# A router chain in program order, its second parts on VectorE, and one modulation sixth moved into it

## The chip, the cores and the metric

One core of a Trainium2 chip runs the whole program. The metric is the device time of one execution in microseconds; the median of three runs before the change is 961.68 us (961.64, 961.68 and 965.34). All arithmetic is float32; "fp32r" in a row marks a float32 operand that TensorE takes in its reduced form, so a value is split into a high part and a remainder and multiplied twice.

## The reference, cut to what matters

Two layers act on 256 latent tokens of width 1024. Layer 0 mixes with attention and a recurrent unit, layer 1 with a Hyena operator (filters applied by Fourier transforms). In each layer the vector `c` gives six modulation vectors, each one sixth of `silu(c) @ ada_w + ada_b`: shift, scale and gate of the mixer (0, 1, 2) and of the expert stage (3, 4, 5). After each mixer comes a mixture of 16 experts:

```
h = rms_norm(x, g) * (1 + sc2) + sh2
s = sigmoid(h @ router_w)            # 16 scores for each token
sel = s + router_b                   # best group of 4, then the best 2 in it
y = sum_e gates[e] * (silu(h @ w1[e]) * (h @ w3[e])) @ w2[e]
x = x + g2 * y
```

## The kernel before, in words

**Stages.** The mixer of layer 0 ends with `project_out` (L501), whose four last steps each finish a quarter of `x`. Between these steps the class `router` (L540) squares, transposes and multiplies the finished quarters. Then comes `moe(0)` (L1171), the Hyena mixer of layer 1 (L1558 on), the second router and `moe(1)`.

**The chain of the router.** `enter` takes the sum of squares and the transposed quarter, `weights` multiplies it with the router's weights, `norm` makes the reciprocal root (a chain of small VectorE instructions, `rstd_of`), `logits` finishes the scores. `split` (L634) writes the normed tokens as a high part `yh` and a remainder `yl`: ScalarE makes `yh` and a full copy, GpSimd subtracts the two. `choose` (L656) finds the two experts of each token by comparisons on VectorE, `count` (L675) numbers the tokens of each expert with small matmuls, `place` (L1197) makes the matrix `P` that picks tokens, and `gather` (L1207) multiplies `yh` and `yl` with `P`. Only then can `up` (L1241) start with the first experts.

**Expert weights.** One expert has six tiles of 1 MB, 96 tiles a layer. They are loaded from SyncE's queue (SP), which issues in order: each load waits until its buffer is free. The buffers are a ring of nine (`w`), which the mixers' and the modulation's weights use as well, the tiles `sp` that the mixers leave free, and an extra pool `x`. The order of loading is the list that `plan` fills (L206 to L308); `emit` issues from it ahead of use.

**The modulation sixths.** `ada_step` (L408) does one of eight steps of a sixth. By PLAN a half goes to VectorE ("V", eight instructions at L440 and L442) or to TensorE ("P", L433, sixteen instructions of the trace a half, and one copy at L437). Its four weight tiles stay in the ring until the last step that reads them. `ada_columns` (L367, for shifts and scales) or `ada_row` (L381, for gates) then finish it on TensorE. `bg(n)` takes n steps beside other work; sixth (1, 4) runs in the mixer of layer 0, (1, 2) and (1, 5) in the Hyena mixer.

**Order.** A planner that simulates the program puts each engine's instructions in order, except inside `in_order("...")`, where the engines named keep the order of the program. Before, that holds for ScalarE and VectorE during `choose` and the second `split` (L623 to L626, CH is 2).

Of the kernel before, what the change touches and what calls it, by code (L numbers as in the profile page):

```python
# [17 lines left out]
D = 1024  # L18
KD = 8
# [41 lines left out]
FILLS = 40  # L61
PLAN = {(0, 3): "VV", (1, 2): "VV", (1, 5): "VV"}
TIN = 0
ADAP = (1, 2, 3, 5)
BGP = (0, 0, 1, 1, 1, 1)

# [100 lines left out]
def build(tc, A, dbg=None, stop=None):  # L167
# [130 lines left out]
    for n in range(6):  # L298
        if n in EARLY:
            plan_moe(1, EARLY[n])  # L300
        for kk in range(2):
            plan(("odin", n, kk), mat(A["od_w_in"][0], kk * 512, 4, n * 512, 512), (128, 4, 512))
        for i in range(4):
            if ADAP[i] == n:
                plan_ada(1, 2 if i < 2 else 5, (i % 2,))
# [96 lines left out]

    todo, ripe, current, ada_alloc, part = [], [], [], [None], [None]

# [3 lines left out]
    def ada_step():  # L408
        for r in ripe:
            r[0] += 1  # L410
        if ripe and ripe[0][0] > LAG:
            l, s, use, e = ripe.pop(0)[1]
            for hf in range(2):
                if use == "row":
                    ada_row(l, s, hf, e[:, hf, :])
                else:
                    ada_columns(l, s, hf, use, e[:, hf, :], ones, 1)
        if not current:
            if not todo:
                return bool(ripe)  # L420
            current.extend([todo.pop(0), 0, ada_alloc[0]("e", 2, 512)])
        (l, s, use), k, e = current
# [3 lines left out]
        for hf in range(2):  # L426
            eh = e[:, hf, :]
            if on[hf] == "P":
                if k == 3:
                    part[0] = ps()  # L430
                if k % 4 == 3:
                    for q in range(4):
                        T.matmul(part[0][32 * q:32 * q + 32, :], cs[:, k - 3 + q, :],  # L433
                                 get(("ada", l, s, hf, k // 4))[:, q, :], start=(k == 3), stop=(k == 7),
                                 tile_position=(0, 32 * q))
                if k == 7:
                    S.activation(eh, part[0], AF.Copy)  # L437
# [12 lines left out]
        if current[1] == KD:  # L450
            if use == "row":
                for hf in range(2):
                    r = l * 12 + s * 2 + hf
                    V.scalar_tensor_tensor(e[0:24, hf, :], adab, ident[0:24, r:r + 1], e[0:24, hf, :], op0=OP.mult,
                                           op1=OP.add)
            ripe.append([0, (l, s, use, e)])
            current.clear()
# [82 lines left out]
    class router:  # L540
# [34 lines left out]
        def weights(self, i):  # L575

            t, n = divmod(i, 2)
            if n == 0:
                self.p[t] = ps()
            for k in range(4):  # L580
# [12 lines left out]
        def run(self, out):  # L593

            self.weigh()
            next(out)
            for i in range(4):
                if i == 2:
                    self.norm(0)
# [5 lines left out]
                if i == 2:  # L605
                    self.logits(0)
            self.norm(1)
            self.weights(3)
            self.logits(1)
            self.y = [eight(n, 2, D, dt=F32R) for n in ("yh", "yl")]  # L610
            if CH == 0:
                self.choose()
                self.split(0)
                self.split(1)
            elif CH == 1:
                self.split(0)
                in_order("A")
                self.choose()
                self.split(1)
                in_order()  # L620
            elif CH == 2:
                self.split(0)
                in_order("AD")  # L623
                self.choose()
                self.split(1)
                in_order()  # L626
            elif CH == 3:
                in_order("A")
                self.choose()
                self.split(0)  # L630
                self.split(1)
                in_order()

        def split(self, t):  # L634

            yh, yl = self.y
            for n in range(2):
                c = slice(n * 512, n * 512 + 512)
                S.activation(yh[:, t, c], x[:, t, c], AF.Copy, scale=self.r[t])
                v = self.alloc()  # L640
                S.activation(v, x[:, t, c], AF.Copy, scale=self.r[t])
                G.tensor_tensor(yl[:, t, c], v, yh[:, t, c].bitcast(F32), op=OP.subtract)

# [12 lines left out]
        def choose(self):  # L656
# [75 lines left out]
        def gates(self):  # L732

            s, msk, gate, sm = self.s, self.msk, self.gate, self.sm
            V.tensor_tensor(gate, s, msk, op=OP.mult)
            V.tensor_reduce(sm[:, 2, 0:2], gate, axis=mybir.AxisListType.X, op=OP.add)
# [38 lines left out]
    with ExitStack() as pa:  # L775
# [38 lines left out]
        later(1, 3, "sh")  # L814
        later(1, 4, "sc")

# [334 lines left out]
        bg_all()  # L1151
        dump("x1", x)

# [17 lines left out]
    def moe(l, route, ws, filler=None, fills=((0, 0, 0),) * 8, budget=0, late=None, prepare=None, finish=None):  # L1171
# [4 lines left out]

        in_order(ORDER[1 + 2 * l])
        steps = filler(wk, f2) if filler else iter(())
        next(steps, None)
        sc, sh, gate, (yh, yl) = route.sc, route.sh, route.gate, route.y  # L1180
# [25 lines left out]

        def gather(d, plan):  # L1207

            P = place_[d]
            e = xe[d] = wk.tile([128, KD, 256], F32, tag="xe", name=nm("xe"))  # L1210
            w = 128 * len(plan[2 * d:2 * d + 2])
            for k2 in range(4):
                p = ps()
                for kk in range(2):
                    k = 2 * k2 + kk
                    for i in range(4):
                        t = i // 2
                        T.matmul(p[:, kk * w:kk * w + w], (yl if i % 2 else yh)[:, t, k * 128:k * 128 + 128],  # L1218
                                 P[:, t, :w], start=(i == 0), stop=(i == 3))
                k = 2 * k2  # L1220
# [102 lines left out]
        place(0, route.pos, firsts)  # L1323
        route.gates()
        gather(0, firsts)
        route.sort(w2("srt"))
# [231 lines left out]
    later(1, 2, "row")  # L1558
    later(1, 5, "row")
    with ExitStack() as ph:  # L1560
# [209 lines left out]
```

## Time and profile before

| | |
|---|---|
| median of three runs | 961.68 us |
| the profiled execution | 964.56 us, span 962.8 us |
| TensorE (PE) busy | 868.0 us, 90% |
| VectorE (DVE) busy | 477.8 us, 50% |
| ScalarE (ACT) busy | 231.9 us, 24% |
| GpSimd (POOL) busy | 25.9 us, 3% |
| moved by DMA | 289.33 MB, mean 301 GB/s |
| mean granted TensorE clock | 0.961 |

All durations in the rows come from this one execution. Times are from the span's start. The mixer of layer 0 ends near 258 us, its experts near 540, the Hyena mixer near 704, the experts of layer 1 at the end. A DMA share of 1.0 means that the core's 16 DMA engines were busy all the time. A clock of 1.0 is 2.4 GHz, 0.5 is 1.2 GHz.

### The profile page before, as it was taken

To read this page: it belongs to the slowest core of one execution; us is meant where nothing else is said; L and a number is where in the kernel's file an instruction comes from. 1 tells how busy PE (TensorE), PEld (TensorE's weight loads), DVE (VectorE), ACT (ScalarE), POOL (GpSimd) and SP (SyncE) were. 2 spreads that over 40 slices of the span, in tenths; PEclk is the share of its full clock that TensorE was granted. 3 is DMA by queue.
4 is the path that set the end of the run, shared out by engine and by line. 5 is a ranking of instruction groups with operands and counts; after the bars stand their busy time and mean duration, and the time that the engine had idled before them with its cause. 6 is when DMAs were issued, how large, how long until landed. Compare 5 with 4: busy or idle time off the path is not lost. (4 is left out here: it accounts for less than half of the span.)

```text
span 962.8 us, 10887 instructions
## 1 busy us (share of the span) xinstructions
PE 868.0 (90%) x3992; PEld 458.1 (48%) x3992; DVE 477.8 (50%) x1119; ACT 231.9 (24%) x451; POOL 25.9 (3%) x29
## 2 busy tenths in 40 slices
PE   3898999999969999889999599999959999988984
PEld 1445755575543543433343288677545352422431
DVE  5349775763364445345622469976163241322123
ACT  3266414430231222122211312211031020100112
POOL 0000000000010000001100000000020000000000
PEclk9899999998969999999999799999978999999997
DMA  9946679469479889999999866842285999999994
GB/s 353 336 183 240 224 263 354 166 223 367 170 271 324 333 324 386 383 400 396 391 362 347 308 228 253 314 167 88 87 298 189 391 396 386 401 392 396 396 386 148
DMA packets 130568, 289.33 MB, mean 301 GB/s; under 512 B 6828, under 2 KB 8876, under 8 KB 130500
## 3 DMA queue, kind: packets, MB, share of 16 engines
q1 hardware_dynamic: 129428, 286.39, 81.5%
q10 hardware_dynamic: 1072, 2.10, 0.7%
q8 instruction: 35, 0.57, 0.2%
q14 instruction: 33, 0.27, 0.1%
HBM read 287.42 MB, written 1.05 MB: 300 GB/s over the span
## 5 line engine op out<-in xcount | busy, mean ns | idle before, releaser
L1247 PE MATMUL ps<-w,xe 128*64 128x512 f32 (+1 forms) x696 | 174.3, 597 | 2.8 <-DMA w<-in_moe_w 2.8
L1247 PEld LDWEIGHTS ps<-w,xe 128*64 128x64 f32 (+1 forms) x696 | 50.0, 129 | 88.0 <-issue 79.2
L1275 PE MATMUL ps<-w,at 128*64 128x512 f32 (+1 forms) x344 | 87.1, 597 | 4.5 <-DMA w<-in_moe_w 2.7
L1591 PE MATMUL ps<-xt,w 128*128 128x256 f32 x384 | 88.2, 388 | 1.8 <-ACT xt L1554 1.8
L1591 PEld LDWEIGHTS ps<-xt,w 128*128 128x128 f32 x384 | 74.2, 195 | 14.4 <-ACT xt L1554 2.1
L1294 DVE TENSOR_TENSOR x<-x,ps 128x512 f32<-128x512 f32 x56 | 37.0, 684 | 68.1 <-PE ps L1292 68.1
L442 DVE SCALAR_TENSOR_TENSOR e<-w,sg,e 128x512 f32<-128x512 f32 x91 | 67.0, 746 | 5.2 <-DMA w<-in_ada_w 4.1
L1281 DVE SCALAR_TENSOR_TENSOR ye<-ps,gs,grow 128x512 f32<-128x512 f32 x28 | 21.0, 748 | 83.9 <-PE ps L1275 83.9
L1247 PE MATMUL ps<-sp,xe 128*64 128x512 f32 (+1 forms) x216 | 55.5, 600 | 1.5 <-DMA sp<-in_moe_w 1.5
L1275 PEld LDWEIGHTS ps<-w,at 128*64 128x64 f32 (+1 forms) x344 | 26.9, 130 | 50.8 <-issue 40.3
L1283 ACT ACTIVATE yeh<-ye 128x512 fp32r<-128x512 f32 x28 | 17.6, 630 | 118.2 <-DVE ye L1281 118.2
L1257 DVE TENSOR_TENSOR th<-th,ps 128x512 f32<-128x512 f32 x14 | 9.6, 688 | 60.5 <-PE ps L1247 60.5
L1247 PE MATMUL ps<-x,xe 128*64 128x512 f32 (+1 forms) x112 | 37.5, 596 | 1.6 <-DMA x<-in_moe_w 1.6
L1218 PE MATMUL ps<-P,yh 128*128 128x256 f32 (+1 forms) x128 | 35.9, 313 | 2.8 <-DVE P L1203 2.8
L1218 PE MATMUL ps<-P,yl 128*128 128x256 f32 (+1 forms) x128 | 35.0, 307 | 0.0
L1223 ACT ACTIVATE xe<-ps,modc 128x256 f32<-128x256 f32 (+1 forms) x32 | 16.5, 540 | 70.0 <-DVE xe L1221 69.9
L1218 PEld LDWEIGHTS ps<-P,yh 128*128 128x128 f32 x128 | 27.9, 218 | 9.6 <-issue 7.1
L844 PE MATMUL ps<-hT,w 128*128 128x512 f32 x64 | 31.0, 643 | 1.2 <-DMA w<-in_ev_w_in 1.2
L1247 PEld LDWEIGHTS ps<-sp,xe 128*64 128x64 f32 (+1 forms) x216 | 16.0, 132 | 28.1 <-issue 24.4
L510 PE MATMUL ps<-w,x 128*128 128x512 f32 x64 | 28.4, 595 | 0.7 <-ACT x L1605 0.7
L510 PE MATMUL ps<-w,mix 128*128 128x512 f32 x64 | 28.8, 598 | 0.0
L1218 PEld LDWEIGHTS ps<-P,yl 128*128 128x128 f32 x128 | 27.8, 217 | 1.7 <-issue 1.7
(350 smaller groups left out, 1313.9 us busy)
## 6 DMA issues: line engine op xcount, KB each, us to landing
w<-in_moe_w SPq DMA_DIRECT2D x126, 1024.0 KB, 13.8
w<-in_ada_w SPq DMA_DIRECT2D x48, 1024.0 KB, 7.1
sp<-in_moe_w SPq DMA_DIRECT2D x41, 1024.0 KB, 14.2
x<-in_moe_w SPq DMA_DIRECT2D x21, 1024.0 KB, 14.5
w<-in_od_w_in SPq DMA_DIRECT2D x12, 1024.0 KB, 7.1
w<-in_ev_w_in SPq DMA_DIRECT2D x4, 1024.0 KB, 11.0
w<-in_ev_w_out SPq DMA_DIRECT2D x4, 1024.0 KB, 6.8
w<-in_moe_w SPq DMA_DIRECT2D x8, 512.0 KB, 9.8
```

Source lines behind the costliest of these rows:

```text
L442: V.scalar_tensor_tensor(eh, w[hf], c, eh, op0=OP.mult, op1=OP.add)
L510: T.matmul(po[t][n], a[:, k, t * 128:t * 128 + 128], b[:, n * 512:n * 512 + 512], start=(k == korder[0] and i == 0), stop=(k == korder[-1] ...
L844: T.matmul(uxp[b], get(("wux", hf))[:, k % 4, b * 128:b * 128 + 128], hT[hf][:, k % 4, :], start=(k == 0), stop=(k == KD - 1))
L1218: T.matmul(p[:, kk * w:kk * w + w], (yl if i % 2 else yh)[:, t, k * 128:k * 128 + 128], P[:, t, :w], start=(i == 0), stop=(i == 3))
L1223: S.activation(e[:, k, :w], p[:, w:2 * w], AF.Identity, scale=sc[:, k:k + 1], bias=sh[:, k:k + 1])
L1247: T.matmul(p[room * i:room * i + room, :], xe[j // 2][:, k, o:o + room], weight(nme, e, k), start=(k == 0), stop=(k == KD - 1), tile_posit ...
L1257: V.tensor_tensor(act[j], act[j], hid[j, "w3"], op=OP.mult)
L1275: T.matmul(p[room * i:room * i + room, :], act[j][:, o:o + room], weight("w2", e, k, n), start=(k == 0), stop=(k == 3), tile_position=(0, ...
L1281: V.scalar_tensor_tensor(e, po[j, n], gs[j], grow[l, 5][:, n * 512:n * 512 + 512], op0=OP.mult, op1=OP.mult)
L1283: S.activation(h, e, AF.Copy)
L1294: V.tensor_tensor(xs, xs, p, op=OP.add)
L1591: T.matmul(pb, w[:, k % 4, b * 128:b * 128 + 128], hT[:, k, :], start=(k == 0 and b % 2 == 0), stop=(k == KD - 1 and b % 2 == 1))
```

## The change

The router's part from the second norm to the gather keeps program order on TensorE, ScalarE and VectorE (`in_order("PAD")`). GpSimd leaves it: `high` writes `yh` on ScalarE, and `low_` makes `yl` in one VectorE instruction for each quarter, the first token half while `count` runs on TensorE, the second behind `place`. `gather` takes all `yh` first and `yl` last, in four PSUM banks at once. The sigmoid's scaling is folded into the bias `rbh`. `gates` and the first step of `filters` move behind the gather. Sixth (1, 4) leaves the mixer of layer 0 and (1, 5) the Hyena mixer; each is now wholly on TensorE, inside the chain, in front of `count`, and finished behind the gather. Their weight tiles are loaded ahead of the experts' and keep four places of the ring until then.

```diff
-PLAN = {(0, 3): "VV", (1, 2): "VV", (1, 5): "VV"}
+PLAN = {(0, 3): "VV", (1, 2): "VV", (1, 4): "PP", (1, 5): "PP"}
-ADAP = (1, 2, 3, 5)
-BGP = (0, 0, 1, 1, 1, 1)
+ADAP = (1, 2)
+BGP = (0, 0, 1, 1, 0, 0)
...
     for k0 in range(0, 8, 2):
         plan(("odo", k0), mat(A["od_w_out"][0], k0 * 128, 2, 0, 1024), (128, 2, 1024))
+    plan_ada(1, 5)
     plan_moe(1)
...
+    rbh = kp.tile([128, 16], F32, name="rbh")
+    V.tensor_scalar(rbh, pc("rb", 0, 16), 0.5, None, op0=OP.add)
...
         def norm(self, t):
-            V.tensor_tensor(self.ss[:, 2 * t:2 * t + 1], self.ss[:, 2 * t:2 * t + 1], self.ss[:, 2 * t + 1:2 * t + 2],
-                            op=OP.add)
-            self.r[t] = rstd_of(self.ss[:, 2 * t:2 * t + 1], 1, D)
+            self.r[t] = rstd_of(self.ss[:, 2 * t + 1:2 * t + 2], 1, D, part=self.ss[:, 2 * t:2 * t + 1])
...
+            self.y = [eight(n, 2, D, dt=F32R) for n in ("yh", "yl")]
             self.norm(1)
+            self.high(0)
+            in_order("PAD")
             self.weights(3)
             self.logits(1)
...
+            S.activation(self.s, self.logit, AF.Tanh, scale=0.5)
+            self.high(1)
+            self.choose()
+
+        def high(self, t):
+            for n in range(2):
+                c = slice(n * 512, n * 512 + 512)
+                S.activation(self.y[0][:, t, c], x[:, t, c], AF.Copy, scale=self.r[t])
+
+        def low_(self, t):
+            for n in range(2):
+                c = slice(n * 512, n * 512 + 512)
+                V.scalar_tensor_tensor(self.y[1][:, t, c], x[:, t, c], self.r[t], self.y[0][:, t, c].bitcast(F32),
+                                       op0=OP.mult, op1=OP.subtract)
...
-            S.activation(s, self.logit, AF.Tanh, scale=0.5)
-            V.tensor_scalar(s, s, 0.5, 0.5, op0=OP.mult, op1=OP.add)
-            V.tensor_tensor(sel, s, pc("rb", 0, 16)[:, None, :].to_broadcast([128, 2, 16]), op=OP.add)
+            V.scalar_tensor_tensor(sel, s, 0.5, rbh[:, None, :].to_broadcast([128, 2, 16]), op0=OP.mult, op1=OP.add)
...
             p = ps()
+            self.low_(0)
             T.matmul(p[:, 0:16], tri, msk[:, 0, :], start=True, stop=True)
...
-        later(1, 4, "sc")
...
-    emit(5)
+    emit(9)
...
+            for i in range(4 if late_low else 0):
+                y_, t = (yh, yl)[i // 2], i % 2
+                for k in range(KD):
+                    T.matmul(pk2[k // 2][:, k % 2 * w:k % 2 * w + w], y_[:, t, k * 128:k * 128 + 128], P[:, t, :w],
+                             start=(i + k % 2 == 0), stop=(i == 3 and k % 2 == 1))
...
+        ada_alloc[0] = lambda n, *shape: [w2(n) for _ in range(2)]
+        later(*(1, 4, "sc") if l == 0 else (1, 5, "row"))
+        bg(KD)
         route.count()
         place(0, route.pos, firsts)
+        route.low_(1)
+        gather(0, firsts, True)
+        in_order(ORDER[1 + 2 * l])
+        next(steps, None)
+        bg_all()
         route.gates()
-        gather(0, firsts)
         route.sort(w2("srt"))
...
-    later(1, 5, "row")
...
-        emit(WHERE.index("x") - sum(EARLY.values()))
+        emit(4 + WHERE.index("x") - sum(EARLY.values()))
```

## Rows read from the trace of the kernel before

**Rows 1.** Busy time by stretch: length, engines with counts, clock, DMA share, GB/s

```profile
222.00:258.00 36.00, 36.00 (x141) 18.50 (x134) 9.13 (x18) 2.37 (x6) 0.00 (x0) 0.99 0.67 251
...
283.00:291.00 8.00, 8.00 (x41) 2.99 (x39) 0.31 (x2) 0.77 (x2) 0.00 (x0) 1.00 0.29 95
291.00:333.00 42.00, 41.82 (x216) 19.45 (x216) 19.48 (x51) 7.80 (x16) 1.71 (x2) 1.00 0.97 357
333.00:345.00 12.00, 12.00 (x59) 4.76 (x56) 3.63 (x9) 2.17 (x4) 0.00 (x0) 1.00 0.48 160
...
670.00:704.00 34.00, 34.00 (x120) 18.12 (x119) 8.72 (x16) 3.34 (x8) 0.00 (x0) 1.00 0.21 66
704.00:723.00 19.00, 8.66 (x62) 8.51 (x61) 14.82 (x68) 8.67 (x18) 5.10 (x4) 0.68 1.01 380
723.00:735.00 12.00, 12.00 (x61) 7.84 (x62) 4.88 (x19) 2.64 (x5) 0.00 (x0) 0.80 0.05 8
735.00:945.00 210.00, 193.30 (x942) 76.35 (x939) 54.43 (x106) 23.69 (x47) 0.00 (x0) 1.00 1.03 392
```

**Rows 2.** Waits, whole span: who waited for whom, us in total, times, longest

```profile
PE ps L679 <- DVE rg L673: 17.8, 2, 8.9
```

**Rows 3.** Timeline of the router chain of layer 1: start, length, engine, line, operation

```profile
709.48 0.23 DVE L590 SCALAR_TENSOR_TENSOR rg<-ps,rs,rwb 128x16 f32<-128x16 f32 x1
709.52 5.17 POOL L642 TENSOR_TENSOR yl<-xT,yh 128x512 fp32r<-128x512 f32 x4 [229.68 <-DMA w<-in_moe_w]
...
710.58 0.21 ACT L663 ACTIVATE rg<-rg 128x32 f32<-128x32 f32 x1
...
710.82 1.24 DVE L664 TENSOR_SCALAR rg<-rg 128x32 f32<-128x32 f32 x1 [1.10 <-ACT rg L663]
...
712.32 1.25 DVE L649 TENSOR_TENSOR cmp<-rg 128x128 f32<-128x128 f32 x1
...
714.76 0.28 DVE L652 TENSOR_TENSOR cmp<-cmp,kc 128x128 f32<-128x128 f32 x1
...
717.83 0.58 PE L679 MATMUL ps<-rg,kc 128*128 128x16 f32 x2 [8.92 <-DVE rg L673]
...
721.53 0.55 PE L1218 MATMUL ps<-P,yh 128*128 128x256 f32 x1 [1.42 <-DVE P L1203]
...
728.25 1.08 PE L1247 MATMUL ps<-sp,xe 128*64 128x512 f32 x4
```

**Rows 4.** Timeline of VectorE in the router chain of layer 0

```profile
267.01 0.29 DVE L649 TENSOR_TENSOR cmp<-rg 128x128 f32<-128x128 f32 x1
...
267.42 1.36 DVE L652 TENSOR_TENSOR cmp<-cmp,kc 128x128 f32<-128x128 f32 x1
```

**Rows 5.** Page, costliest groups: busy, mean ns, idle before

```profile
L442 DVE SCALAR_TENSOR_TENSOR e<-w,sg,e 128x512 f32<-128x512 f32 x91 | 67.0, 746 | 5.2 <-DMA w<-in_ada_w 4.1
```

**Rows 6.** Timeline of TensorE: first and next instruction of a later gather, layer 0

```profile
324.59 0.39 PE L1218 MATMUL ps<-P,yh 128*128 128x256 f32 x1
...
328.53 0.38 PE L1234 MATMUL ps<-kc,P 128*128 128x128 f32 x2
```

**Rows 7.** Timeline of TensorE at the end of the mixer of layer 0

```profile
230.33 1.92 PE L433 MATMUL ps<-w,cs 128*32 128x512 f32 x16
...
237.44 1.84 PE L370 MATMUL ps<-ones,e 128*128 128x1 f32 x16
```

**Rows 8.** Waits of TensorE, 300 to 545 us

```profile
PE ps L1247 <- DMA w<-in_moe_w: 1.9, 1, 1.9
PE ps L1275 <- DMA w<-in_moe_w: 1.3, 2, 0.7
```

**Rows 9.** Chain that ended last, 670 to 722 us: start, length, piece

```profile
676.03 1.72 PE ps L385 x4
```

**Rows 10.** Waits of TensorE, 545 to 705 us

```profile
PE ps L1495 <- DVE x L1665: 0.9, 1, 0.9
```

**Rows 11.** Timeline of SyncE's queue at the router of layer 0

```profile
259.28 8.20 SPq L219 DMA_DIRECT2D sp<-in_moe_w  x5
```

More of the change, by code (lines that the diff above doesn't have):

```diff
@@ L302, in build @@
             plan(("odin", n, kk), mat(A["od_w_in"][0], kk * 512, 4, n * 512, 512), (128, 4, 512))
-        for i in range(4):
+        for i in range(2):
             if ADAP[i] == n:
-                plan_ada(1, 2 if i < 2 else 5, (i % 2,))
+                plan_ada(1, 2, (i,))
     for k0 in range(0, 8, 2):
         plan(("odo", k0), mat(A["od_w_out"][0], k0 * 128, 2, 0, 1024), (128, 2, 1024))
+    plan_ada(1, 5)
     plan_moe(1)
@@ L399, in ada_first @@
         return e
-    todo, ripe, current, ada_alloc, part = [], [], [], [None], [None]
+    todo, ripe, current, ada_alloc, part = [], [], [], [None], {}
     def later(l, s, use):
@@ L414, in ada_step @@
                 if use == "row":
-                    ada_row(l, s, hf, e[:, hf, :])
+                    r = l * 12 + s * 2 + hf
+                    V.scalar_tensor_tensor(e[hf][0:24], adab, ident[0:24, r:r + 1], e[hf][0:24], op0=OP.mult, op1=OP.add)
+                    ada_row(l, s, hf, e[hf])
                 else:
-                    ada_columns(l, s, hf, use, e[:, hf, :], ones, 1)
+                    ada_columns(l, s, hf, use, e[hf], ones, 1)
         if not current:
@@ L420, in ada_step @@
                 return bool(ripe)
-            current.extend([todo.pop(0), 0, ada_alloc[0]("e", 2, 512)])
+            e = ada_alloc[0]("e", 2, 512)
+            current.extend([todo.pop(0), 0, e if isinstance(e, list) else [e[:, hf, :] for hf in range(2)]])
         (l, s, use), k, e = current
@@ L426, in ada_step @@
         for hf in range(2):
-            eh = e[:, hf, :]
+            eh = e[hf]
             if on[hf] == "P":
                 if k == 3:
-                    part[0] = ps()
+                    part[hf] = ps()
                 if k % 4 == 3:
                     for q in range(4):
-                        T.matmul(part[0][32 * q:32 * q + 32, :], cs[:, k - 3 + q, :],
+                        T.matmul(part[hf][32 * q:32 * q + 32, :], cs[:, k - 3 + q, :],
                                  get(("ada", l, s, hf, k // 4))[:, q, :], start=(k == 3), stop=(k == 7),
@@ L436, in ada_step @@
                 if k == 7:
-                    S.activation(eh, part[0], AF.Copy)
+                    S.activation(eh, part[hf], AF.Copy)
             elif on[hf] == "V":
@@ L450, in ada_step @@
         if current[1] == KD:
[L451 to L455, printed above, removed]
             ripe.append([0, (l, s, use, e)])
@@ L579, in weights @@
                 self.p[t] = ps()
+                V.tensor_scalar(self.ss[:, i:i + 1], self.ss[:, i:i + 1], 1.0 / D, EPS, op0=OP.mult, op1=OP.add)
             for k in range(4):
@@ L597, in run @@
             for i in range(4):
-                if i == 2:
-                    self.norm(0)
                 if i < 3:
@@ L605, in run @@
                 if i == 2:
+                    self.norm(0)
                     self.logits(0)
+            self.y = [eight(n, 2, D, dt=F32R) for n in ("yh", "yl")]
             self.norm(1)
+            self.high(0)
+            in_order("PAD")
             self.weights(3)
             self.logits(1)
[L610 to L636, printed above, removed]
+            S.activation(self.s, self.logit, AF.Tanh, scale=0.5)
+            self.high(1)
+            self.choose()
+        def high(self, t):
             for n in range(2):
                 c = slice(n * 512, n * 512 + 512)
[L639 to L642, printed above, removed]
+                S.activation(self.y[0][:, t, c], x[:, t, c], AF.Copy, scale=self.r[t])
[4 more added lines that the diff above has]
+                                       op0=OP.mult, op1=OP.subtract)
         def rank(self, v, n, out):
@@ L734, in gates @@
             s, msk, gate, sm = self.s, self.msk, self.gate, self.sm
+            V.tensor_scalar(s, s, 0.5, 0.5, op0=OP.mult, op1=OP.add)
             V.tensor_tensor(gate, s, msk, op=OP.mult)
@@ L1149, in build @@
         route0 = router(0, lambda: t4("xT", 512))
+        bg_all()
         route0.run(out)
-        bg_all()
-        dump("x1", x)
     def extra(nx):
@@ L1205, in place, with gather @@
                                     pos[:, t, es_[0]:es_[0] + n, None].to_broadcast([128, n, room]), op=OP.is_equal)
-        def gather(d, plan):
+        def gather(d, plan, late_low=False):
             P = place_[d]
@@ L1211, in gather @@
             w = 128 * len(plan[2 * d:2 * d + 2])
-            for k2 in range(4):
[L1213 to L1219, printed above, removed]
+            pk2 = [ps() for _ in range(4)] if late_low else {}
+            for i in range(4 if late_low else 0):
[3 more added lines that the diff above has]
+                             start=(i + k % 2 == 0), stop=(i == 3 and k % 2 == 1))
+            for k2 in range(4):
+                if late_low:
+                    p = pk2[k2]
+                else:
+                    p = ps()
+                    for kk in range(2):
+                        k = 2 * k2 + kk
+                        for i in range(4):
+                            t = i // 2
+                            T.matmul(p[:, kk * w:kk * w + w], (yl if i % 2 else yh)[:, t, k * 128:k * 128 + 128],
+                                     P[:, t, :w], start=(i == 0), stop=(i == 3))
                 k = 2 * k2
```

3 lines of the change are left out of this document (1 added, 2 removed).

## Prediction

> **What bounds the kernel now.** I read the stretches of busy time first, since the shares over the whole span mix stages with different limits. In the last 36 us of the mixer of layer 0 TensorE has no gap (36.00 of 36.00) and DMA is busy 0.67 of the time: TensorE bounds it [rows 1]. The end of the Hyena mixer, 670 to 704, is the same (34.00 of 34.00) with DMA at 0.21. From 735 to 945 it is the other way: DMA share 1.03 at 392 GB/s, TensorE with 16.7 us of gaps, so the experts of layer 1 end when their weights have come. Layer 0's experts lie between: DMA has free time in three stretches (0.29 of 283 to 291, 0.97 of 291 to 333, 0.48 of 333 to 345), and later TensorE waits for weights three times, 3.2 us in all [rows 8]. Both engines run level there, and whoever comes later sets the end.
>
> The list of waits then gives the places that the change is about: twice TensorE waits 8.9 us for the last comparison of the router [rows 2]. The timeline shows why that lasts so long. While GpSimd subtracts (709.52 to 714.69), VectorE instructions of 0.28 or 0.29 us take 1.24 to 1.25 us, L664 and L649 in layer 1 [rows 3]; in layer 0 L649 is quick (0.29) and L652 takes 1.36 [rows 4]. Rule and row can be held together here: the Trainium skill, "SBUF — State Buffer", section "Who interferes with whom", says that a VectorE instruction with two inputs in SBUF is held up by a GpSimd one that reads SBUF. By that rule the new VectorE subtraction, which has two such inputs, would suffer as well if GpSimd ran beside it; in the chain nothing is left on GpSimd, so it changes no term below.
>
> **The chain, step by step (layer 1's rows).** Removed on the path: the scores are ready at 709.48 + 0.23 = 709.71, the tanh starts at 710.58 because ScalarE copies first, and now it stands ahead of the second copies: 0.8 us. L664 and the addition behind it take 710.82 to 712.32, 1.50 us; one instruction replaces them, estimated at 0.23 by L590, which has the same operation: 1.27 us. L649 and L650 take 712.32 to 714.76, 2.44 us; undisturbed they take 0.41 (267.01 to 267.42): 2.03 us. The sum is 4.1 us [rows 3, 4]. Layer 0 has the same wait of 8.9 us with other instructions slowed; I take 4.1 there too.
>
> Added on the path: `low_` is four VectorE instructions of the form of L442, 0.75 us each [rows 5]. The first two (1.5 us) lie between the last comparison and the counting's end, a stretch in which VectorE waits for the count; count and placing take 3.7 us in all (717.83 to 721.53). The second two run behind `place` and are wanted by the last quarter of the gather, which takes 6.7 us (721.53 to 728.25) when the clock is low and 3.9 us (324.59 to 328.53) when it is high [rows 3, 6]: even then they have 2.9 us. If that cover failed, 1.5 us a layer would come on top. Queued behind them on VectorE are the gather's evacuations, wanted only later. As all four banks now finish in the last quarter, I charge 0.5 us for the first evacuation before `up` (nearest row: none shows it; 0 to 1.1).
>
> The sixth's own work: a half on TensorE is 16 instructions, 1.92 us [rows 7], so two halves take 3.8 us. They stand in front of the count, where TensorE still waits 8.9 - 4.1 = 4.8 us: hidden, and 3.8 us on the path if the wait were gone. Its finish behind the gather is not hidden: 1.84 us for columns in layer 0 [rows 7], 1.72 for the row in layer 1 [rows 9].
>
> The clock: 0.68 over 704 to 723 and 0.80 over 723 to 735 [rows 1], so the first gather runs partly at 1.2 GHz. With 3.8 us of 512-column matmuls in the gap it may stay at 2.4 GHz; that is worth 0 to 2.8 us (6.7 against 3.9). I take 0.7, near the lower end, because the count's small matmuls and two short waits still lie in front of the gather. In layer 0 then: 4.1 - 1.8 - 0.5 + 0.7 = 2.5 us earlier (1.8 to 4.6).
>
> The shorter norm, the constant `rbh`, the scaling that moves into `gates` and the first step of `filters` are one small instruction each way or lie beside the gather: 0 (-0.2 to 0.3).
>
> **The mixer of layer 0** loses the 16 instructions of L433 and 16 of L370: 1.92 + 1.84 = 3.8 us of an engine without gaps, so all of it counts [rows 1, 7]. The eight VectorE instructions that go (6 us) were hidden: VectorE is busy 9.13 of 36 us.
>
> **Layer 0's experts.** TensorE thus starts them 3.8 + 2.5 = 6.3 us earlier. But the sixth's four weight tiles keep four of the nine ring places until the chain, so four expert tiles load later: at 392 GB/s a tile of 1 MB takes 2.67 us, four 10.7 us. DMA's free time that can take them is 0.71 x 8 + 0.03 x 42 + 0.52 x 12 = 5.7 + 1.3 + 6.2 = 13.2 us [rows 1]. The stream is then 2.5 us ahead, with the mixer's 3.8 us 6.3 us: the same number. I take 6.3 us for the end of this stage. Ends: if only the first free stretch can be used, 10.7 - 5.7 - 3.8 = 1.2 us later than before; if the waits of 3.2 us go too and the clock stays high, 3.8 + 4.6 + 3.2 = 11.6 us earlier.
>
> **The Hyena mixer** loses the row's 1.72 us on TensorE, which had no gap there [rows 1, 9], and 16 VectorE instructions, 12 us. VectorE's work was hidden but for one wait of 0.9 us [rows 10]. I take 1.7 us (to 2.6). The four tiles that no longer load in it had time enough.
>
> **Layer 1's experts** end with DMA, so what the chain gains counts only as far as weights flow earlier. Before, the queue stands still from 723 to 735 (0.05 busy): 11.4 us [rows 1]. The four tiles that are now loaded behind the chain take 10.7 us, and with the loads of 704 to 723 ahead of them there is work from 704 on without a gap. Net 0.7 us; with the gap's edges I take 1.0 (0.7 to 1.8). The 4.1 us of this chain themselves are worth nothing: TensorE will wait longer in the last passes.
>
> **Sum.** 6.3 + 1.7 + 1.0 = 9.0 us off the profiled execution's 964.56, which is a span of 962.8 and 1.8 around it: 955.6. The median of the three runs is 961.68, 2.9 lower; taken from that, 952.7. About 0.5%, 4.8 us, is what a measurement of this kernel can tell from no change.
>
> **Rivals.** *The held places cost more (A).* Free time from 333 to 345 may come from the order in which tiles become free, not from a full buffer. Then layer 0 ends 1.2 us later, and 1.7 + 1.0 remain: 1.5 us, 960.2. For it: TensorE does wait for weights later [rows 8]; against it: TensorE starts earlier and asks earlier for everything.
> *More than the sum (B).* Clock high, waits gone: 11.6 + 2.6 + 1.8 = 16.0 us, 945.7. For it: the matmuls in the gap; against it: DMA at 0.97 from 291 on.
> *The queue stands behind the held tiles (C), slower.* SyncE issues in order. If the four loads that need the sixth's places stand ahead of the five expert tiles issued from 259.28 [rows 11], these wait for the sixth's matmuls and for 10.7 us of loading. The matmuls end 8.7 us after the mixer (layer 1: 717.83 - 8.92 + 3.8 = 712.7 against 704). In layer 0 the first pair of tiles then lands near 258 - 3.8 + 8.7 + 10.7 + 5.3 = 279 and the second near 284, where `up` began 24 us after the mixer (728.25 against 704), near 282: all that mixer and chain gave is lost, 1 us later than before. In layer 1 the same order leaves DMA idle between the loads near 704 and 712.7, some 5 us, less the 1.0: 4 us. With 1.7 from the Hyena mixer the whole is 3.3 us slower: 965.0. It decides as soon as a held place precedes a free one in the queue. Against it: a planner orders that queue by when buffers come free.
> *The chain does not do what it says (D).* If `low_` lands on the path in layer 0 (1.5 + 1.5) and the clock stays low, its 2.5 us are gone; TensorE gains 3.8 of the mixer, then 1.7 and 1.0: 955.2.
>
> **How the numbers follow.** Forecast 0.45 (948 to 957), A 0.17, B 0.20, C 0.10, D 0.08. Faster by over 0.5% (below 956.9): 0.42 + 0.20 + 0.04 = 0.66; slower by over 0.5% (above 966.5): half of C and some of A, 0.08; the rest, 0.26, within. The range 944 to 963 leaves out most of C and the far end of B.
>
> **What would show it.** Right: no GpSimd rows in the chains, L649 at 0.29 us, the wait of L679 under 5 us with L433 rows in front of it; DMA without a gap from 704 to 945 and none near 285; L385 only once in the Hyena mixer. Wrong: a DMA gap at 705 to 712, `up` waiting for tiles `sp` in layer 0, a DMA-bound end of layer 0 that has not moved, or TensorE gaps in the mixers that the trace of before lacks.

## The result, and the profile after

The changed kernel takes 952.97 us (median of 4 runs, 950.47 to 955.92) against 961.66 for the one before in the same comparison; the ratio is 0.990, 95% interval 0.988 to 0.992. A second comparison gave 0.9898 (0.9880 to 0.9916). The forecast was 952.7. The profiled execution went from 964.56 to 955.92 us, 8.64 less where the sum said 9.0.

Busy time by stretch of the kernel after, the same stretches and columns as in [rows 1]:

```profile
222.00:258.00 36.00, 36.00 (x133) 19.63 (x130) 6.68 (x19) 5.14 (x13) 0.00 (x0) 0.97 0.47 172
283.00:291.00 8.00, 8.00 (x39) 2.66 (x36) 1.81 (x7) 0.87 (x2) 0.00 (x0) 1.00 1.06 388
291.00:333.00 42.00, 41.82 (x214) 19.37 (x211) 19.17 (x49) 7.84 (x16) 1.63 (x2) 1.00 1.03 385
333.00:345.00 12.00, 12.00 (x58) 5.51 (x57) 7.03 (x15) 3.36 (x6) 0.73 (x1) 1.00 0.76 290
704.00:723.00 19.00, 16.71 (x102) 9.55 (x95) 15.40 (x68) 5.19 (x11) 0.00 (x0) 0.88 1.02 388
723.00:735.00 12.00, 11.19 (x54) 3.73 (x50) 1.38 (x2) 0.60 (x1) 0.00 (x0) 1.00 1.05 393
735.00:945.00 210.00, 190.69 (x911) 74.34 (x910) 56.95 (x107) 25.80 (x53) 0.00 (x0) 1.00 1.00 378
```

The last column but one is to be read against [rows 1]: DMA's free time at 283 to 291 (0.29 before) and its standstill at 723 to 735 (0.05) are gone, and GpSimd has no instruction in either chain. The chain of layer 0 on TensorE (start, length, operation, and in brackets the idle time before and who ended it):

```profile
258.12 1.98 PE L584 MATMUL ps<-rws,xT 128*128 128x16 f32 x16
260.02 3.64 PE L437 MATMUL ps<-w,cs 128*32 128x512 f32 x32
264.80 0.37 PE L665 MATMUL ps<-rg,kc 128*128 128x16 f32 x2 [1.14 <-DVE rg L658]
267.60 1.38 PE L1199 MATMUL ps<-P,yh 128*128 128x256 f32 x8 [1.53 <-DVE P L1186]
276.35 1.08 PE L1239 MATMUL ps<-sp,xe 128*64 128x512 f32 x4
```

The wait of 8.9 us [rows 2] is gone but for 1.1: the chain is 4.2 us shorter, and the sixth's 32 matmuls fill 3.6 of the rest. VectorE in the chain of layer 1:

```profile
703.25 0.29 DVE L636 TENSOR_TENSOR cmp<-rg 128x128 f32<-128x128 f32 x1
703.46 0.29 DVE L637 TENSOR_TENSOR cmp<-rg 128x128 f32<-128x128 f32 x1
703.75 0.29 DVE L639 TENSOR_TENSOR cmp<-cmp,kc 128x128 f32<-128x128 f32 x1
706.48 0.19 DVE L658 TENSOR_TENSOR rg<-rg,sm 128x32 f32<-128x32 f32 x1
706.59 1.41 DVE L628 SCALAR_TENSOR_TENSOR yl<-x,rs,yh 128x512 fp32r<-128x512 f32 x2
```

The first comparison, L649 before, took 1.25 us [rows 3] and takes 0.29 now (L636); the new subtractions begin behind the chain's last instruction (L658).

### The profile page after: what moved, and what is told of

It reads as the page before. It is cut to its first block, busy times and chain, and to the rows that moved or that the text cites. A ratio compares the mean times of both kernels' runs of the same rounds, so it can differ in the third digit from the quotient of the medians.

```text
span 954.1 us, 10948 instructions
## 1 busy us (share of the span) xinstructions
PE 874.8 (92%) x4040; PEld 457.0 (48%) x4040; DVE 458.9 (48%) x1104; ACT 228.6 (24%) x446; POOL 15.7 (2%) x21
## 5 line engine op out<-in xcount | busy, mean ns | idle before, releaser
L1239 PE MATMUL ps<-w,xe 128*64 128x512 f32 (+1 forms) x696 | 173.5, 597 | 2.6 <-DMA w<-in_moe_w 2.6
L1239 PEld LDWEIGHTS ps<-w,xe 128*64 128x64 f32 (+1 forms) x696 | 49.9, 129 | 87.8 <-issue 79.1
L1239 PE MATMUL ps<-sp,xe 128*64 128x512 f32 (+1 forms) x216 | 54.8, 598 | 1.4 <-DMA sp<-in_moe_w 1.4
L446 DVE SCALAR_TENSOR_TENSOR e<-w,sg,e 128x512 f32<-128x512 f32 x70 | 51.5, 746 | 3.5 <-DMA w<-in_ada_w 2.8
L1239 PE MATMUL ps<-x,xe 128*64 128x512 f32 (+1 forms) x112 | 37.5, 596 | 1.6 <-DMA x<-in_moe_w 1.6
L1239 PEld LDWEIGHTS ps<-sp,xe 128*64 128x64 f32 (+1 forms) x216 | 16.0, 132 | 30.2 <-issue 26.8
L1267 PE MATMUL ps<-sp,at 128*64 128x512 f32 (+1 forms) x112 | 27.4, 599 | 3.0 <-ACT at L345 1.7
L512 PE MATMUL ps<-w,x 128*128 128x512 f32 x64 | 28.4, 595 | 0.7 <-ACT x L1603 0.7
L512 PE MATMUL ps<-w,mix 128*128 128x512 f32 x64 | 28.9, 603 | 0.0
L1244 ACT ACTIVATE th<-ps 128x512 f32<-128x512 f32 x14 | 8.4, 597 | 82.3 <-PE ps L1239 66.8
L1277 DVE TENSOR_TENSOR yel<-ye,yeh 128x512 fp32r<-128x512 f32 x28 | 19.3, 691 | 16.7 <-ACT yeh L1275 10.4
L437 PE MATMUL ps<-w,cs 128*32 128x512 f32 x160 | 27.3, 689 | 0.0
```

The costliest lines, as they stand in the source:

```text
L437: T.matmul(part[hf][32 * q:32 * q + 32, :], cs[:, k - 3 + q, :], get(("ada", l, s, hf, k // 4))[:, q, :], start=(k == 3), stop=(k == 7), t ...
L512: T.matmul(po[t][n], a[:, k, t * 128:t * 128 + 128], b[:, n * 512:n * 512 + 512], start=(k == korder[0] and i == 0), stop=(k == korder[-1] ...
L1239: T.matmul(p[room * i:room * i + room, :], xe[j // 2][:, k, o:o + room], weight(nme, e, k), start=(k == 0), stop=(k == KD - 1), tile_posit ...
L1267: T.matmul(p[room * i:room * i + room, :], act[j][:, o:o + room], weight("w2", e, k, n), start=(k == 0), stop=(k == 3), tile_position=(0, ...
L1277: V.tensor_tensor(o, e, h.bitcast(F32), op=OP.subtract)
```

## Experiments

All are judged by two things: the time against the kernel before on the same chip, and the length of stages on TensorE, read from the timelines. "Mixer" is the end of the last output projection (L512 in the kernel after), "count" the first matmul of the router's count (L665), "up" the first matmul of the first pass (L1239). The stages come from one profile of each kernel. Times in us; "below before" goes by the ratios.

| kernel | ratio to before (95%) | mixer 0 to count | mixer 0 to up | up to end of experts 0 | Hyena mixer | its end to up | up to end |
|---|---|---|---|---|---|---|---|
| before | 1 | 13.8 | 23.4 | 269.4 | 152.6 | 24.1 | 234.6 |
| after | 0.990 | 9.5 | 21.1 | 269.9 | 151.1 | 20.8 | 235.9 |
| after_b (the same) | 0.9898 (0.9880–0.9916) | 9.5 | 21.1 | 267.8 | 150.6 | 21.7 | 235.3 |
| chain_only | 0.9952 (0.9935–0.9969) | 9.8 | 19.7 | **272.4** | 153.0 | 18.9 | 235.7 |
| sixths_only | 1.0020 (1.0004–1.0037) | **16.2** | 29.1 | 269.3 | 151.3 | 25.6 | 234.4 |
| only14 | 0.9914 (0.9894–0.9933) | 9.5 | 21.1 | 269.5 | 152.6 | 19.5 | 235.0 |
| only15 | 0.9958 (0.9940–0.9975) | 9.8 | 19.2 | **271.6** | 151.2 | 21.2 | 235.8 |
| chain_hold | 0.9924 (0.9905–0.9943) | 9.7 | 19.7 | 268.8 | 151.6 | 19.6 | 235.4 |
| after_gp | 1.0012 (1.0002–1.0023) | **13.6** | 26.9 | 269.1 | 149.9 | 26.5 | 235.6 |
| after_warm | 0.9888 (0.9871–0.9904) | 11.0 | 19.8 | 269.9 | 151.2 | 19.2 | 237.4 |
| only14_warm | **0.9862** (0.9837–0.9887) | 11.0 | 19.8 | 267.9 | 152.2 | 18.3 | 236.3 |
| only14_warm_late | 0.9885 (0.9859–0.9910) | 11.0 | 18.5 | 270.1 | 151.3 | 19.6 | 235.8 |
| nogp | 0.9927 (0.9905–0.9949) | 11.2 | 21.5 | 267.8 | 152.5 | 20.7 | 234.5 |

The median of before was 963.2 to 963.3 us in these comparisons, so 0.001 is about 1 us. A stage of one profile moves by 1 to 2 us without a cause (the two profiles of the changed kernel show how much).

**chain_only**: the sixths are put back where they were, with the lists and `emit` counts that belong to them (not shown).

```
-        later(*(1, 4, "sc") if l == 0 else (1, 5, "row"))
-        bg(KD)
         route.count()
...
+        later(1, 4, "sc")       # mixer of layer 0
+    later(1, 5, "row")          # Hyena mixer
```

> The new router chain alone; both modulation sixths stay where the kernel before has them. Theory T (both expert stages end when their weights have come; the quicker chain and the moved sixths draw on the same idle DMA time): layer 0 starts its experts 4.2 us earlier and ends them 3.6 us earlier. In layer 1 the queue stands still from 723 to 735 before because its ring is full until the first up projection frees a place; that start comes 4 us earlier, so the standstill is about 4 us shorter and the end 3.9 us earlier. Sum 7.5 us less than before, near 954.2. Rival R1 (as the prediction has it, layer 1's chain is worth nothing, and the parts add up): only layer 0's 4.2 us, near 957.5, and this run and sixths_only sum to the 8.7 us of the whole. Rival R2 (TensorE's start counts in full in both layers): 8.4 us, near 953.3; it differs from T in sixths_only.

Measured: 4.6 us below before, 958.71. That is near R1's number, but not in R1's place: the chain itself gives what was expected in both layers, the experts of layer 0 then take 3 us longer, and layer 1 ends 4.0 us sooner behind the Hyena mixer. **sixths_only**: the router of before, with the sixths' three lines added ahead of its count, and their loads and their finish as in the kernel after.

> The router chain of before, GpSimd's subtractions included; only the two sixths are moved onto TensorE in the chain's wait. T: 3.5 us off the mixer, 1.8 to 2.9 of them lost behind the gather, so layer 0 ends about 1 to 1.6 us earlier; 1.5 from the Hyena mixer; layer 1's queue has the four held tiles to load where it stood still, 1.9. Sum 5.0 us less than before (3.5 to 7), near 956.7, and with chain_only's 7.5 together 12.5, well over the 8.7 of the whole change: what they share is layer 1's standstill. R1 (additive): 4.5 us, such that the two sum to 8.7. R2 (starts of TensorE count in full, the stream does not matter): 3.5 + 1.5 less 1.8 and 1.7 behind the gathers, 1.5 us.

Measured: 965.11, 1.9 us *slower* than before. The two halves sum to 2.7 us, the whole gives 9.8: my first theory (shared idle time, so the sum exceeds the whole) has the wrong sign, and so has the additive rival. The halves need each other, and by the table nearly all of that lies in layer 0 of sixths_only: from the mixer's end to the end of the experts it takes 298.5 us, against 292.8 before, 292.1 in chain_only and 291.0 in the kernel after. On TensorE there:

```profile
257.93 5.33 PE L437 MATMUL ps<-w,cs 128*32 128x512 f32 x30
263.19 1.07 PE L580 MATMUL ps<-rws,xT 128*128 128x16 f32 x8
270.39 0.58 PE L678 MATMUL ps<-rg,kc 128*128 128x16 f32 x2 [5.15 <-DVE rg L672]
```

Without the written order the planner puts 30 of the sixth's matmuls ahead of the last router weights (L580), and VectorE waits 4.8 us for these: the count starts 16.2 us behind the mixer instead of 13.8. From the count to up it takes another 12.9 us instead of 9.6, with the sixth's columns in the gather.

**only14** and **only15** move one sixth each.

```
-        later(*(1, 4, "sc") if l == 0 else (1, 5, "row"))
-        bg(KD)
+        if l == 0:              # only15: if l == 1, with (1, 5, "row")
+            later(1, 4, "sc")
+            bg(KD)
```

> The new chain, and only layer 0's sixth, (1, 4), moved into the chain; (1, 5) stays in the Hyena mixer on VectorE with its row behind. T: layer 0 as in the whole change, 5.3 us; the Hyena mixer 0; in layer 1 the ring is full before the chain as before, and the standstill is shorter by the chain's 4 us: 3.9. Sum 9.2 us, near 952.5: no worse than the whole change. R1: the whole change without what came from (1, 5), which is 1.5 in the Hyena mixer and 1.9 at the end of layer 1: 5.3 us, near 956.4.

> The new chain, and only layer 1's sixth, (1, 5), moved into the chain; (1, 4) stays in the mixer of layer 0. T: layer 0 by the chain alone, 3.6 us; Hyena mixer 1.5; layer 1 as in the whole change, 1.9. Sum 7.0 us, near 954.7; the queue in layer 1 has no standstill. If layer 0's sixth gave its 3.8 us of the mixer in full: 5.2 us only, near 956.5. If it cost layer 0 by the held places more than it gave: over 8.7 us, below 953.

Measured: 954.36 and 959.32, 8.3 and 4.0 us below before. only14 comes near T, only15 stays below every expectation. So (1, 4) is worth some 4 us beside the chain, (1, 5) next to nothing. after_b was to tell the same of (1, 5) beside (1, 4): a ratio of 0.986 if it is worth the forecast's 2.7 us, 0.990 to 0.991 if nothing to 1.2. Measured: 0.9898, 1.5 us better than only14, with overlapping intervals. What (1, 4) does is seen in layer 0 of chain_only, on TensorE, in a stretch of busy time (columns as [rows 1]) and in SyncE's queue:

```profile
277.02 1.08 PE L1239 MATMUL ps<-sp,xe 128*64 128x512 f32 x4
282.14 2.46 PE L1239 MATMUL ps<-sp,xe 128*64 128x512 f32 x6 [2.72 <-DMA sp<-in_moe_w]
```

```profile
248.00:255.00 7.00, 7.00 (x17) 3.04 (x16) 2.84 (x6) 0.72 (x2) 0.00 (x0) 1.00 0.00 0
```

```profile
255.21 2.52 SPq L219 DMA_DIRECT2D w<-in_moe_w  x2
257.77 9.67 SPq L219 DMA_DIRECT2D sp<-in_moe_w  x5
```

The same queue in the kernel after:

```profile
253.15 2.52 SPq L219 DMA_DIRECT2D w<-in_moe_w  x2
255.72 8.46 SPq L219 DMA_DIRECT2D sp<-in_moe_w  x5
269.10 10.65 SPq L219 DMA_DIRECT2D w<-in_moe_w  x4
```

The five tiles `sp` are the first that the first pass reads, and they are issued only at the mixer's end. In chain_only nine expert tiles `w` are issued ahead of them; the quicker chain starts up at 277.02, and TensorE then waits 2.7 us for its second group. In the kernel after the sixth holds four of the ring's places, so four of these `w` tiles go behind `sp`, and up does not wait. I took the one for the cause of the other (theory T2, below). The rows speak against it: in chain_only DMA is idle from 248 to 255, so seven of the nine tiles have landed long before, and in both kernels just two `w` tiles are issued next, and `sp` 0.4 us behind the mixer's end (257.33 and 255.27).

**chain_hold** tests T2 by itself: the sixth is still computed in the mixer, but its four tiles are kept.

```
+        if l == 0:
+            hold = ps()
+            for a in range(4):
+                T.matmul(hold[:, a:a + 1], get(("ada", 1, 4, a % 2, a // 2))[:, 3, :128], ones[:, 0:1], start=True, stop=True)
         route.count()
```

> chain_only, with the sixth (1, 4) still computed in the mixer, but its four weight tiles kept in the ring until the chain by four one-column matmuls whose result nobody reads. New theory T2: in chain_only the up projection starts at 277.02 and waits 2.7 us, since the five tiles sp of the first pass stand behind four expert tiles that nobody needs yet; in the whole change the held places push those four behind. So here the second group of up matmuls finds its tile: no wait there, no second clock dip at 282 to 286, and layer 0 ends 2 to 4 us earlier than in chain_only (549.41, mixer end 257.33): 6 to 9 us below before in all against chain_only's 4.6. Rival (what chain_only lacks is the sixth's TensorE work in the mixer): as chain_only, 4.6 below before; or later, if the four tiles that load late are missed.

Measured: 955.62, 7.3 us below before and 2.7 less than chain_only, with intervals that overlap (0.9905 to 0.9943 and 0.9935 to 0.9969). The time came out as T2 has it, but its reason is not borne out. Up's second group still waits for `sp`, as it does in only15, which holds nothing in layer 0 (chain_hold, then only15):

```profile
282.10 2.39 PE L1239 MATMUL ps<-sp,xe 128*64 128x512 f32 x10 [1.23 <-DMA sp<-in_moe_w]
```

```profile
283.84 1.98 PE L1240 MATMUL ps<-sp,xe 128*64 128x512 f32 x4 [1.85 <-DMA sp<-in_moe_w]
```

The mixers end at 258.78 and 260.36, so the group starts 23.3 and 23.5 us behind the mixer's end, 24.8 in chain_only. From it to the end of the experts it is 265.2 us in chain_hold and 267.3 in both others, but 267.8 and 265.7 in the two profiles of the changed kernel, which differ in nothing. That held places bring the `sp` tiles sooner is not shown, and what brings the 2.7 us stays open.

What the traces do show is that the second group follows the chain only in part. It starts 25.1 us behind the mixer's end before and 23.2 to 23.5 in after, after_b, only14, only15 and chain_hold, though up's first group starts anywhere from 19.2 to 21.1. So part of the quicker chain is lost there; only the kernels with added matmuls, further below, have it at 21.6 to 21.9. The sixth's columns, which delay the first group by 1.4 us, then cost nothing at the second, while without the sixth the mixer itself ends 3.4 us sooner (mean over the kernels): that accounts for most of what (1, 4) is worth. The start of layer 0 in chain_only once more:

```profile
283.00:291.00 8.00, 8.00 (x32) 2.95 (x31) 0.00 (x0) 0.06 (x1) 0.00 (x0) 0.81 0.29 99
```

The clock is 0.81 there (1.00 in the kernel after and in chain_hold): it fell behind the wait. A cost of that does not show in the stage's length from the second group on.

**after_gp** puts four GpSimd subtractions a layer back beside the new chain, two behind each `high`, of which nothing is read.

```
+                G.tensor_tensor(self.alloc(), x[:, t, c], self.y[0][:, t, c].bitcast(F32), op=OP.subtract)
```

> The changed kernel with four GpSimd subtractions put back beside the chain; their result is unread, no instruction waits for them. The chain's gain was split in the prediction into order (0.8), one instruction for two (1.27) and VectorE unhindered (2.03). If the third is real, VectorE's comparisons take 1.2 us again where they overlap, the count of both layers starts 2 to 4 us later, and the whole is 1.5 to 3 us slower than the changed kernel, by layer 0 alone. If GpSimd's work had been harmless: same starts, same time.

Measured: 964.63, 10 us slower than the kernel after, where 1.5 to 3 were expected, and 1.2 slower than before. Its GpSimd and VectorE in layer 0:

```profile
260.29 2.51 POOL L630 TENSOR_TENSOR xT<-x,yh 128x512 f32<-128x512 f32 x2 [257.73 <-ACT yh L624]
264.10 2.55 POOL L630 TENSOR_TENSOR xT<-x,yh 128x512 f32<-128x512 f32 x2 [1.30 <-ACT yh L624]
```

```profile
260.35 1.23 DVE L485 SCALAR_TENSOR_TENSOR rs<-rs 128x1 f32<-128x1 f32 x1
261.61 1.20 DVE L491 SCALAR_TENSOR_TENSOR rs<-rs 128x1 f32<-128x1 f32 x1
264.17 1.36 DVE L647 TENSOR_TENSOR cmp<-cmp,kc 128x128 f32<-128x128 f32 x1
265.57 1.24 DVE L648 TENSOR_TENSOR cmp<-cmp 128x128 f32<-128x128 f32 x1
```

Four subtractions of 1.26 us, four VectorE instructions held for about as long; undisturbed they take 0.15 to 0.29, so this is 4.1 us, all of the chain's gain. The count is 4.1 us later behind the mixer than in the kernel after, and up 5.8 in layer 0 and 5.7 in layer 1.

**nogp** is the kernel before with this alone: the subtraction goes to VectorE.

```
-                v = self.alloc()
-                S.activation(v, x[:, t, c], AF.Copy, scale=self.r[t])
-                G.tensor_tensor(yl[:, t, c], v, yh[:, t, c].bitcast(F32), op=OP.subtract)
+                V.scalar_tensor_tensor(yl[:, t, c], x[:, t, c], self.r[t], yh[:, t, c].bitcast(F32),
+                                       op0=OP.mult, op1=OP.subtract)
```

> The kernel before, with one change: the low parts are four VectorE instructions instead of four ScalarE copies and four GpSimd subtractions; norm, order, tanh, sixths as before. after_gp has shown that GpSimd's four subtractions beside the new chain cost about 4.1 us a layer, as much as the chain gained. If they are the whole of it, the count of both layers starts 9.5 to 10.5 us behind the mixer (13.75 before), and the time is that of chain_only: 0.995 of before, since layer 0's first tiles are late here too. If order, the joined instruction and the shorter norm are a real part (2.1 of 4.1 in the prediction), the count starts 11.5 to 12 behind the mixer and 2 us are gained: 0.998.

Measured: 956.32, 7.0 us below before, better than either expectation: this edit alone brings most of the whole, and no less than chain_only, the intervals overlapping. The count starts 11.2 us behind the mixer, 2.5 sooner. That is net, for two of the new subtractions land inside the chain, here in layer 0, where L483 and L489 wait for them:

```profile
262.93 0.15 DVE L489 SCALAR_TENSOR_TENSOR rs<-rs 128x1 f32<-128x1 f32 x1
263.00 0.75 DVE L640 SCALAR_TENSOR_TENSOR yl<-x,rs,yh 128x512 fp32r<-128x512 f32 x1
263.66 0.21 DVE L483 SCALAR_TENSOR_TENSOR rs<-rs 128x1 f32<-128x1 f32 x1
263.79 0.75 DVE L640 SCALAR_TENSOR_TENSOR yl<-x,rs,yh 128x512 fp32r<-128x512 f32 x1
264.45 0.15 DVE L489 SCALAR_TENSOR_TENSOR rs<-rs 128x1 f32<-128x1 f32 x1
265.17 0.18 DVE L663 TENSOR_SCALAR rg<-rg 128x32 f32<-128x32 f32 x1 [0.29 <-ACT rg L662]
```

From L489 to L483 and on to L489 it takes 0.73 and 0.79 us here, 0.19 and 0.26 in the same chain undisturbed (layer 1 before): 1.1 us. So GpSimd's absence is worth about 3.6 us of the 4.2, and the new order, which has these two subtractions beside the count, the joined instruction and the norm some 1.7, of which 1.1 only undoes that loss. (The four ScalarE copies go as well; in layer 0 the chain did not wait for them.) Up starts 1.9 us sooner behind the mixer in layer 0 and 3.4 sooner behind the Hyena mixer in layer 1, 5.3 of the 7.0; the rest lies within what stages move by. Nine `w` tiles are issued ahead of `sp` here too, and up's second group starts 23.8 us behind the mixer, without a wait, though its first starts 1.8 us later than in chain_only.

**after_warm** and **only14_warm** add matmuls whose result is not read in TensorE's waits.

```
+        warm_ = ps()
+        for _ in range(1 - l):  # only14_warm: 1 if l == 0 else 3
+            T.matmul(warm_, ones, x[:, 0, 0:512], start=True, stop=True)
         route.count()
+        for _ in range(1 + l):  # only14_warm: 1
+            T.matmul(warm_, ones, x[:, 0, 0:512], start=True, stop=True)
```

> The changed kernel with idle 128x512 matmuls (result unread) in TensorE's two waits of the chain: one before the count and one before the gather in layer 0, two before the gather in layer 1. If the clock stays at 1.0 for the gather of layer 0 (0.50 from 268 to 274 in the changed kernel), up starts 3 to 4 us earlier than 276.35 and the whole is 2 to 4 us quicker where the first tiles are there in time, 0 to 1 where they are not. If the clock falls all the same, the time is that of the changed kernel or 1 us more.

> only14 with idle matmuls in TensorE's waits of both chains (layer 0: one before the count, one before the gather; layer 1: three and one). Theory T3, from the stage times of the runs so far: from the first up matmul to the end of layer 1's experts it is 234.4 to 235.9 us in ten of eleven profiles, so up's start counts in full there unless the queue runs without a gap; after_warm, where (1, 5) is loaded behind the chain, has 237.4 and no gap. Here the queue has its gap, so the quicker gather counts: layer 0 about 1.4 us as after_warm against after_b, layer 1 about 2.5. That is 3.9 below only14: ratio to before 0.987, near 950.5 where before is 963.2. Rival (the weight stream limits layer 1 in any case): as after_warm, 0.9888 or above.

The gather of layer 0 in after_b, and then in after_warm (columns as [rows 1]):

```profile
269.00:276.00 7.00, 7.00 (x37) 7.00 (x38) 5.42 (x30) 0.21 (x1) 0.00 (x0) 0.57 1.05 371
```

```profile
268.00:276.00 8.00, 7.04 (x53) 5.89 (x52) 7.90 (x40) 0.95 (x3) 0.00 (x0) 1.00 1.05 374
```

The clock stays at 1.00 and the gather with the sixth's columns takes 6.1 us instead of 8.7. But the count starts 1.4 us later behind the mixer, in all three kernels with such matmuls: the clock has been low before, at 260 to 264 in after_warm, and the sixth's own matmuls took 5.34 us instead of 3.64:

```profile
260.00:264.00 4.00, 4.00 (x25) 1.07 (x28) 3.26 (x18) 2.59 (x6) 0.00 (x0) 0.57 1.02 367
```

This lies ahead of the first added matmul (265.20), so that the low clock cannot be their doing directly; what sets the moment is not settled. The rest of the delay is that matmul itself: with the sixth running late it no longer fits into the wait, and the count starts only 0.96 us behind its start (266.16). Layer 1 is the cleaner case, since the clock was low at 700 to 705 with and without them (0.69 in the kernel after, 0.66 in after_warm). Its gather, 710 to 716, in the kernel after and then in after_warm:

```profile
710.00:716.00 6.00, 5.18 (x19) 3.30 (x20) 5.93 (x31) 1.19 (x2) 0.00 (x0) 0.72 1.04 407
```

```profile
710.00:716.00 6.00, 6.00 (x39) 4.38 (x37) 5.51 (x28) 1.90 (x4) 0.00 (x0) 1.00 1.03 409
```

By the ratios after_warm is 1.0 us better than after_b, with overlapping intervals, where 2 to 4 were expected if the clock stays up. In layer 1 it starts up earlier and then needs 237.4 us, with DMA never idle. only14_warm has idle time there:

```profile
716.00:728.00 12.00, 12.00 (x58) 4.94 (x56) 1.82 (x8) 0.68 (x2) 0.00 (x0) 1.00 0.55 202
728.00:937.00 209.00, 191.15 (x914) 74.69 (x910) 55.53 (x104) 24.76 (x50) 0.00 (x0) 1.00 1.02 383
```

Measured: 950.27, ratio 0.9862, as expected to 0.3 us: the quickest of all, some 3.5 us better than the changed kernel (the two intervals overlap between 0.988 and 0.989).

**only14_warm_late** issues the sixth's columns behind the first up matmuls (`bg_all()` moves behind `slots(1, ...)`).

> only14_warm, and the sixth's columns (16 small matmuls, 1.9 us within layer 0's gather) are issued behind the first up matmuls. If up's start counts in full in layer 0: 1.5 to 1.9 us quicker than only14_warm. If the tiles sp of the first pass now come too late (in chain_hold the second group waits until some 22.9 us behind the mixer's end): up starts earlier and waits 1 to 2 us, the whole stays the same.

Measured: 952.04, ratio 0.9885, its interval overlapping only14_warm's; nothing gained. Up starts 1.3 us sooner and no `sp` is late, but from there the experts take 2.2 us longer, about what a stage moves by. The columns are TensorE's work on either side of up: moved from one side to the other they gain nothing. Neither expectation named this.

## Why the prediction was right, step by step

**Mixer of layer 0, 3.8 us.** It ends at 255.27 instead of 258.77, 3.5. Over the kernels with the sixth in the mixer and those without (five and eight profiles) the mean end differs by 3.4. Right.

**The chain, 4.1 us.** The count starts 4.2 us sooner behind the mixer. Right in size, but the split was not. I gave GpSimd 2.03 and the rest 2.07; nearly all of it is GpSimd's. With its work put back, 4.1 us go (after_gp); without it and without the new order, 2.5 come net and about 3.6 in all (nogp). The slip is in my reading of the rows: I counted L664 among the instructions of 0.28 or 0.29 us and put its 1.24 us into the term of the joined instruction, but its like takes 0.18 where GpSimd is still (nogp, L663), so that 1.06 of that term is GpSimd's too. Each subtraction holds whichever VectorE instruction it meets: the rows of before have L664 and L649 held in layer 1 and L652 in layer 0 [rows 3, 4]. The Trainium skill, "SBUF — State Buffer", section "Who interferes with whom", has it that VectorE and GpSimd share a port pair with an exclusive lock, and that a VectorE instruction with two inputs in SBUF contends there with a GpSimd one that reads SBUF. The four held ones of after_gp agree. L664 [rows 3] has one input and took 1.24 us; by the same section of the Trainium skill a tensor_scalar can contend as well, in a mode that takes both ports, and no run shows whether this one ran in it.

**Gather and columns.** I forecast 2.5 us of layer 0's chain left at up (4.1 - 1.8 - 0.5 + 0.7); 2.3 are. The size held, two terms did not: the columns take 2.8 us instead of 1.8 (2.09 and 0.72, after_b), for the clock did not help. It is 0.57 over 269 to 276 in after_b, as shown, and 0.62 over 276 to 282 before.

**Layer 0's experts, 6.3 us.** They ended 5.3 us sooner (546.24 against 551.52). The number held, the reason beside it did not. I set TensorE's start against a stream that four later tiles put 10.7 us back, read the three waits for weights of 3.2 us [rows 8] as the stream's limit, and got 6.3 twice. The table says otherwise: where the first tiles are there, it is 267.8 to 270.1 us from up to the end, wherever up starts; the waits for tiles `w` from 300 to 540 us are 2.6 to 3.3 us in all thirteen profiles, whether up started at 273 or 283. A wait of constant size moves with its engine; it is not a limit that a sooner start runs into. What can be late is the first pass: its `sp` tiles are issued when the mixer ends, in every kernel but nogp and sixths_only within 0.5 us, and up's second group starts only 1.9 us sooner behind the mixer than before (23.2 against 25.1). Rival C feared for the same tiles, but its condition did not come about: the four loads that need the held places are issued behind `sp` (269.10 against 255.72).

**Hyena mixer, 1.7 us.** 1.5 in the profile (152.6 to 151.1); 1.4 between the means of the kernels with and without (1, 5) there. Right.

**Layer 1's experts, 1.0 us.** 1.9 measured (258.7 to 256.8 from the Hyena mixer's end). "The 4.1 us of this chain themselves are worth nothing" is the step that fails. From up to the end it is 234.4 to 235.9 us in eleven of thirteen profiles, and a sooner start counts for the most part: in chain_only up starts 5.2 us sooner behind the Hyena mixer, and the end of all comes 4.0 us sooner. My reading is that the ring is full when up starts, so that the bytes still to come are the same and a sooner start shortens the standstill before it. The sixth (1, 5) takes some 2 us of that back: from the Hyena mixer's end to the end of all, the new chain needs 256.6 to 257.0 us with it and 254.5 to 255.4 without. Most of this stands at up, which starts at 20.8 to 21.7 us instead of 18.9 to 19.6 in the kernels without added matmuls: the sixth's row lies in front of it, and takes 3.33 us at the low clock (711.85, kernel after) where I had 1.72. That the stream itself, which then has no standstill left, sets the end shows at most in after_warm (237.4). The Hyena mixer gives 1.4 us in return; only14_warm against after_warm, 2.5 us by the ratios though with overlapping intervals, points the same way.

Sum by the profiles: 3.5 + 2.3 - 0.5 + 1.5 + 1.9 = 8.7, where 9.0 was forecast. Layer 0's 1.0 us too much and layer 1's 0.9 too little cancel, and that the median meets the forecast to 0.3 us is luck: the second comparison had 954.55.

What stays open: what brings chain_hold's 2.7 us, and why executions of the changed kernel fall 4 us apart (950.5 and 950.9, 955.0 and 955.9), with a granted clock of 0.98 and 0.97 over the span; in the latter no experiment tells cause from effect.

## What to carry to other kernels

Before counting a quicker chain as gained, look at when the load that its consumer needs can be issued: in layer 0 of chain_only up starts 3.7 us sooner, and 3.0 of these are lost by the stage's end. Compare the length from the first consumer to the stage's end over several variants: if it hardly changes, a sooner start counts, however busy DMA is. When two edits brought 2.7 us one at a time and 9.8 together, the stage lengths told where a half went wrong: look there before calling an edit useless.

## What the runs showed of the hardware that was not expected

A GpSimd subtraction of 128x512 (1.26 us) held one VectorE instruction for about its own length, even one of 128x1 elements (L485: 1.23 us instead of 0.21): in this chain the price went by the number of GpSimd instructions, not by VectorE's sizes. Two matmuls of 512 columns in TensorE's waits (after_warm) went with a granted clock of 1.00 in gathers that otherwise ran at 0.57 and 0.72, in both layers. And an instruction with one input was held beside GpSimd as those with two are (L664, 1.24 us).
